# Seven products of a retention layer: four sets of weight buffers, another order at the exchange of passes, and modulation in rows of 1024 columns

## Chip, cores and metric

The kernel runs on one core of one Trainium2 chip. Its time is the device time of one execution in microseconds; a kernel's time is the median over its runs. One execution is also recorded by the hardware profiler, and all readings of the trace are of that one.

## What is computed

Two decoder layers over 512 tokens of width 2048, in float32. Layer 0 is a retention layer with 8 heads (256 wide for queries and keys, 512 wide for values and gates); layer 1 is latent attention. Each layer's input is normalised and modulated: a shift, a scale and a gate come from a product of the conditioning vector with a 2048 x 6144 matrix per layer.

```python
c_act = jax.nn.silu(c)
for i in range(DEPTH):                      # 2 layers
    mod = (c_act @ ada_w[i] + ada_b[i])[:, None, :]
    shift, scale, gate = jnp.split(mod, 3, axis=-1)
    h = rmsnorm(x, norm_g[i]) * (1.0 + scale) + shift
    y = retention_branch(...) if i % 2 == 0 else mla_branch(...)
    x = x + gate * y
return rmsnorm(x, final_norm_g)

def retention_branch(h, pos, w_in, gn_g, w_out):
    proj = h @ w_in                          # 2048 x 12288: q, k (2048 each), v, g (4096 each)
    q, k, v, g = jnp.split(proj, [RET_QK, 2 * RET_QK, 2 * RET_QK + RET_WIDTH], axis=-1)
    q = rope(q, pos); k = rope(k, pos) * RET_DK ** -0.5
    y = chunkwise_retention(q, k, v)         # 8 heads, chunks of 128 tokens
    y = groupnorm(y) * gn_g
    return (silu(g) * y) @ w_out             # 4096 x 2048

def mla_branch(h, pos, w_in, ...):
    cq, ckv, k_rope, g = split(h @ w_in)     # 512, 512, 64, 2048 columns
    ...                                      # attention over 16 heads
    return (silu(g) * o) @ w_out
```

## The kernel before

Every matrix product is made of three matmuls: both operands are split into a high and a low part in a reduced format (`split`: ScalarE casts the high part, VectorE subtracts it to get the low part), and TensorE adds high x high, high x low and low x high. A weight block therefore goes through a raw buffer (a DMA from the chip's memory), a high and a low buffer; `load_w` does this for plain products. Buffers come from pools by tag with a number of places: `raw`, `whi` and `wlo` have three each, `raw2` three more, `tmp` six. PSUM has four banks `acc` and four `aux`. The program is written in one order; a scheduler then orders the instructions of each engine, and each engine runs its own in that order.

The order of the work: the first pass (queries and keys of head 0, values of head 0, three of four column blocks of its gate, while layer 0's shift and scale are computed); a short stage `g03` for the fourth block; then heads 1 to 7. Queries and keys of a head (`queries_and_keys`) are eight units of 24 matmuls. Values and gates of a head (`values_and_gates`) are a 2 x 2 block product done with seven block products rather than eight: tokens in two halves, columns in values and gates, and the 2048 rows in eight pairs of 128-row blocks. Sums and differences of the activations are formed once (`form_sums`); those of the weights are formed by VectorE for each block. *Pass A* has eight units: each loads the rows of a pair (`e`, in a `raw` buffer, and `o`, in a `raw2` buffer; values and gates side by side), forms three differences, splits, and multiplies into the bank pairs `x`, `s`, `y`, `z` (24 matmuls). At the *exchange* ScalarE copies `x` and `s` away (`m1`, `m5`), VectorE adds `m1` to `y` and then `y + m5` to `s`, and `z` is copied (`m4`). *Pass B* has eight units of 18 matmuls: the odd block again (`p`) and the even block's gates (`q`), multiplied into `x`, `s`, `y`. At the end the results go to the chip's memory.

Beside this work runs the rest of the modulation (`later_modulation`): layer 0's gate, layer 1's shift, scale and gate, 16 pieces of 512 columns. A piece is eight 512 KB transfers (two rows of blocks each, buffer `bw`, two places), each followed by two VectorE steps of 512 columns that add the row times its element of the conditioning vector to `am`. `use_modulation` then sums over partitions by small matmuls into `mod_ps` (L532 for shift and scale, L537 for the gates). `next(later, None)` issues one transfer with its two steps; it is called once per unit of `g03`, of queries and keys and of both passes.

After head 7's values and gates come the query and key products of heads 6 and 7, into which `hooks` puts steps of the retention of heads 0 and 1 (loads and rotations by `rope_halves`, the scores `s`, and so on) at given units; then the output projection with the other heads' retention (also by `hooks`), and layer 1: its input `h2`, the low-rank products `cq` and `ckv`, the gates `g2` in four parts, attention, output projection.

Of the kernel before, what the change touches and what calls it, by code (L numbers as in the profile page):

```python
# [16 lines left out]
P = 128  # L17
T = 512
# [31 lines left out]
def hybrid_trunk_kernel(  # L50
# [225 lines left out]
    def rotary_tables(cos, sin, col, signed, name):  # L276

        pos_i = base.tile([P, T], I32, tag="pos", bufs=1, name=f"{name}_pi")
# [210 lines left out]
    def keep_rows(ps, dst_d, r0, name, func=AF.Identity):  # L489
# [8 lines left out]
    def later_modulation():  # L498
        for i, sect, part in (
            [(0, 2, n) for n in range(4)]  # L500
            + [(1, 0, n) for n in range(4)]
            + [(1, 1, n) for n in range(4)]
            + [(1, 2, n) for n in range(4)]
        ):
            name = f"mod_{i}_{sect}_{part}"
            c0 = sect * D + part * 512
            am = lpp.tile([P, T], F32, tag="bm", bufs=2, name=f"{name}_am")
            for u in range(8):
                aw = lpp.tile([P, 2, T], F32, tag="bw", bufs=2, name=f"{name}_aw{u}")
                nc.sync.dma_start(aw, (ada0, ada1)[i][:, 2 * u : 2 * u + 2, c0 : c0 + 512])  # L510
                for ki in range(2):
                    k = 2 * u + ki
                    if k == 0:
                        DVE.tensor_scalar(
                            out=am, in0=aw[:, 0, :], scalar1=cact[:, 0:1], scalar2=None, op0=ALU.mult
                        )
                    else:
                        DVE.scalar_tensor_tensor(  # L518
                            out=am, in0=aw[:, ki, :], scalar=cact[:, k : k + 1], in1=am, op0=ALU.mult, op1=ALU.add
                        )  # L520
                if u == 7:
                    ripe.append((name, i, sect, part, am))
                yield

    def use_modulation():

        while ripe:
            name, i, sect, part, am = ripe.pop(0)
            ps = aux(f"{name}_ps")
            if sect < 2:  # L530
                for b in range(4):
                    PE.matmul(ps[:, b : b + 1], am[:, b * P : (b + 1) * P], crow, start=True, stop=True)  # L532
# [756 lines left out]
```

## Time and profile before

| | |
|---|---|
| median of 3 runs | 2357.36 us |
| lowest and highest run | 2350.77 and 2358.31 us |
| the profiled execution's own time | 2360.03 us |
| its span in the trace | 2357.8 us |
| mean granted clock of TensorE | 0.977 |
| HBM read, written | 396.46 MB, 50.35 MB |

The stages in the profiled execution, by the first matmul of each: first pass 0 to 183 us; `g03` and queries and keys of head 1 to 247.6; then heads 1 to 7, with queries and keys ahead of values and gates up to head 5, to 1046.7; queries and keys of heads 6 and 7 to 1177.4; output projection of layer 0 to about 1605; layer 1 to the end.

How to read it: a matmul's busy time is modelled, and weight loads of TensorE overlap it, so a busy TensorE is measured best by how many matmuls a stretch holds. A wait is put down to the engine and line that released it last. The granted clock is a share of full speed, averaged over the stretch.

### The profile page before, as it was taken

How to read it: one execution, taken by the hardware profiler on the slowest of the kernel's cores; microseconds unless marked ns; L12 is line 12 of the kernel's file. 1: busy time of each engine (PE TensorE's matmuls, PEld its weight loads, DVE VectorE, ACT ScalarE, POOL GpSimd, SP SyncE). 2: the span in 40 equal slices, each digit the busy share in tenths (PEclk: the TensorE clock that was granted, in tenths of full speed). 3: DMA queues.
4: the chain of work that ended last, by engine and by line, in shares of the span. 5: the costliest groups of instructions: out<-in, count | busy, mean ns of one | idle time of the engine just before them, and what ended most of it. 6: DMA issues, size and time to landing. Idle time of an engine off the chain costs nothing.

```text
span 2357.8 us, 28090 instructions
## 1 busy us (share of the span) xinstructions
PE 2229.0 (95%) x10186; PEld 1832.7 (78%) x10186; DVE 1522.9 (65%) x2373; ACT 1008.5 (43%) x1515; POOL 125.7 (5%) x228
## 2 busy tenths in 40 slices
PE   5999999999999899999899999999999999999997
PEld 4777877777778677777688888787888888888886
DVE  6889968677787866766556567347242257777545
ACT  5563433423233244443345455446232255555333
POOL 0000010000000000010000000001000000000000
PEclk8999999999999999999899999999999999999999
DMA  9977888686888865665555454453334333324433
GB/s 323 330 224 241 291 289 268 218 269 219 274 272 304 267 203 178 215 212 186 180 184 177 163 181 138 150 188 108 90 90 134 108 107 99 90 76 165 163 122 119
DMA packets 259500, 448.67 MB, mean 190 GB/s; under 512 B 21913, under 2 KB 95777, under 8 KB 259361
## 3 DMA queue, kind: packets, MB, share of 16 engines
q1 hardware_dynamic: 244256, 400.62, 53.0%
q0 software_dynamic: 14592, 46.18, 5.1%
q8 instruction: 79, 1.29, 0.2%
q14 instruction: 61, 0.49, 0.1%
q10 hardware_dynamic: 512, 0.08, 0.0%
HBM read 396.46 MB, written 50.35 MB: 190 GB/s over the span
## 4 chain that ended last, share of the span: by engine, by line
PE 46%; issue 27%; DMA 11%; DVE 9%; ACT 4%; POOL 2%; SPq 0%; ACTq 0%; POOLq 0%; DVEq 0%
PE o L160 5%; PE o L162 5%; PE o L161 5%; DMA mod_aw<-in_ada_w_dram 5%; PE g L160 2%; PE g L162 2%; PE g L161 2%; DVE mod_am L518 2%; DMA aw<-in_ada_w_dram 2%; DVE am L399 1%; PE qk L162 1%; PE qk L161 1%; PE qk L160 1%; ACT p L1113 1%; DMA qk_raw<-in_ret_w_in_dram 1%
## 5 line engine op out<-in xcount | busy, mean ns | idle before, releaser
L160 PE MATMUL o<-o_w_hi,o_h 128*128 128x512 f32 x768 | 301.7, 393 | 2.7 <-ACT o L881 2.1
L161 PE MATMUL o<-o_w_lo,o_h 128*128 128x512 f32 x768 | 300.0, 391 | 0.0
L162 PE MATMUL o<-o_w_hi,o_l 128*128 128x512 f32 x768 | 298.6, 390 | 0.0
L135 DVE TENSOR_TENSOR o_w_lo<-o_w_raw,o_w_hi 128x1024 fp32r<-128x1024 f32 x96 | 117.2, 1222 | 161.5 <-ACT o_w_hi L134 161.4
L518 DVE SCALAR_TENSOR_TENSOR mod_am<-mod_aw,cact,mod_am 128x512 f32<-128x512 f32 x240 | 179.4, 747 | 46.3 <-DMA mod_aw<-in_ada_w_dram 44.4
L160 PE MATMUL qk<-hT,qk_hi 128*128 128x512 f32 x448 | 180.2, 402 | 4.4 <-ACT qk_hi L134 4.4
L162 PE MATMUL qk<-hT,qk_lo 128*128 128x512 f32 x448 | 177.5, 400 | 0.1
L161 PE MATMUL qk<-hT,qk_hi 128*128 128x512 f32 x448 | 177.4, 396 | 0.0
L160 PEld LDWEIGHTS o<-o_w_hi,o_h 128*128 128x128 f32 x768 | 144.7, 188 | 34.3 <-ACT o L881 4.1
L162 PEld LDWEIGHTS o<-o_w_hi,o_l 128*128 128x128 f32 x768 | 144.2, 188 | 30.5 <-DVE o_l L135 0.6
L161 PEld LDWEIGHTS o<-o_w_lo,o_h 128*128 128x128 f32 x768 | 144.7, 188 | 29.1
L134 ACT CAST o_w_hi<-o_w_raw 128x1024 fp32r<-128x1024 f32 x96 | 100.9, 1052 | 113.5 <-PE o L162 92.8
L134 ACT CAST qk_hi<-qk_raw 128x1024 fp32r<-128x1024 f32 x64 | 67.1, 1051 | 143.9 <-PE qk L161 102.5
L135 DVE TENSOR_TENSOR g_lo<-g_raw,g_hi 128x1024 fp32r<-128x1024 f32 (+1 forms) x42 | 49.2, 1173 | 116.9 <-ACT g_hi L134 108.2
L134 ACT CAST vg_o_hi<-vg_o 128x1024 fp32r<-128x1024 f32 x56 | 59.0, 1053 | 132.3 <-PE s L623 66.6
L160 PEld LDWEIGHTS qk<-hT,qk_hi 128*128 128x128 f32 x448 | 86.3, 193 | 24.5 <-ACT qk_hi L134 5.2
L162 PEld LDWEIGHTS qk<-hT,qk_lo 128*128 128x128 f32 x448 | 85.9, 192 | 20.4 <-DVE qk_lo L135 1.9
L161 PEld LDWEIGHTS qk<-hT,qk_hi 128*128 128x128 f32 x448 | 86.0, 192 | 19.1 <-issue 1.2
L160 PE MATMUL g<-h,g_hi 128*128 128x512 f32 x256 | 99.8, 390 | 1.1 <-ACT ckv_n L994 1.1
L135 DVE TENSOR_TENSOR o_l<-o_in,o_h 128x1024 fp32r<-128x1024 f32 x40 | 48.9, 1224 | 79.8 <-ACT o_h L134 79.7
L162 PE MATMUL g<-h,g_lo 128*128 128x512 f32 x256 | 99.6, 389 | 0.0
L161 PE MATMUL g<-h,g_hi 128*128 128x512 f32 x256 | 99.6, 389 | 0.0
(425 smaller groups left out, 5461.0 us busy)
## 6 DMA issues: line engine op xcount, KB each, us to landing
mod_aw<-in_ada_w_dram SPq DMA_DIRECT2D x128, 512.0 KB, 4.7
aw<-in_ada_w_dram SPq DMA_DIRECT2D x128, 256.0 KB, 6.0
qk_raw<-in_ret_w_in_dram SPq DMA_DIRECT2D x128, 256.0 KB, 4.2
o_w_raw<-in_ret_w_out_dram SPq DMA_DIRECT2D x64, 512.0 KB, 3.8
vg_o<-in_ret_w_in_dram SPq DMA_DIRECT2D x56, 512.0 KB, 5.0
vg_e<-in_ret_w_in_dram SPq DMA_DIRECT2D x56, 512.0 KB, 4.5
vg_p<-in_ret_w_in_dram SPq DMA_DIRECT2D x56, 512.0 KB, 4.2
g_raw<-in_mla_w_in_dram SPq DMA_DIRECT2D x32, 512.0 KB, 3.6
```

What stands on the lines that cost most here:

```text
L134: ACT.copy(hi, src)
L135: DVE.tensor_sub(lo, src, hi.bitcast(F32))
L160: PE.matmul(o, lhs[0], rhs[0], start=first and not seeded, stop=False, skip_group_check=seeded)
L161: PE.matmul(o, lhs[0], rhs[1], start=False, stop=False, skip_group_check=seeded)
L162: return PE.matmul(o, lhs[1], rhs[0], start=False, stop=last, skip_group_check=seeded)
L399: DVE.scalar_tensor_tensor(out=am, in0=aw[:, j], scalar=ck, in1=am, op0=ALU.mult, op1=ALU.add)
L518: DVE.scalar_tensor_tensor(out=am, in0=aw[:, ki, :], scalar=cact[:, k : k + 1], in1=am, op0=ALU.mult, op1=ALU.add)
L1113: ACT.activation(p_[:, :n], ps[:, :n], AF.Exp, bias=nb, scale=scale, accum_out=sm)
```

## The change

- **Buffer sets.** In `values_and_gates` raw, high and low buffers of a block now belong together as a set. Three sets are the old `raw`, `whi`, `wlo`; every fourth block takes a set of its own (`own_r`, `own_h`, `own_l`). `raw2` is gone, and `st` has four places instead of five. Casts and subtractions are written in another order: both casts of a unit, then both low parts.
- **Exchange.** The last unit of pass A multiplies into `x`, `y`, `s`, `z` in that order. `m1` is added to `y` before `s` is copied. Pass B's unit 0 multiplies into `x` alone; unit 1 into `x` and then unit 0's and its own `y` and `s`; later units into `x`, `y`, `s`.
- **Modulation.** A piece is 1024 columns: 16 transfers of one row of blocks (512 KB as before), each followed by one VectorE step of 1024 columns. Its matmuls are issued only when `use_modulation` has been called twice more since it was complete. Steps are issued two per unit of queries and keys (heads 2 to 5) and at every second unit of pass B, none in pass A as the program is written. The gate of layer 1 is left to layer 1 itself, beside the gates `g2`.
- **Start.** `form_sums` moves into the units of `g03` and queries and keys of head 1; head 0's gate rows are put by in `tmp` buffers; the positions' table shares `tmp`.
- **Hooks.** Retention of heads 0 and 1 is stepped at other units of the query and key products of heads 6 and 7, and head 1's rotated rows go to buffers of their own (`odd`); one table of the output projection changes too.

```diff
@@ keep_rows, later_modulation, use_modulation
-        st = lpp.tile([P, T], F32, tag="st", bufs=5, name=name)
+        st = lpp.tile([P, T], F32, tag="st", bufs=4, name=name) if own is None else own(name)
...
-            c0 = sect * D + part * 512
-            am = lpp.tile([P, T], F32, tag="bm", bufs=2, name=f"{name}_am")
-            for u in range(8):
-                aw = lpp.tile([P, 2, T], F32, tag="bw", bufs=2, name=f"{name}_aw{u}")
-                nc.sync.dma_start(aw, (ada0, ada1)[i][:, 2 * u : 2 * u + 2, c0 : c0 + 512])
-                for ki in range(2):
...
+            c0 = sect * D + part * 1024
+            am = pool.tile([P, 2, T], F32, tag="bm", bufs=2, name=f"{name}_am")
+            for k in range(KD):
+                aw = pool.tile([P, 2, T], F32, tag="bw", bufs=2, name=f"{name}_aw{k}")
+                nc.sync.dma_start(
+                    aw, (ada0, ada1)[i][:, k : k + 1, c0 : c0 + 1024].rearrange("p k (a n) -> p (k a) n", a=2)
+                )
+                ck = cact[:, k : k + 1]
+                if k == 0:
+                    DVE.tensor_scalar(out=am, in0=aw, scalar1=ck, scalar2=None, op0=ALU.mult)
+                else:
+                    DVE.scalar_tensor_tensor(out=am, in0=aw, scalar=ck, in1=am, op0=ALU.mult, op1=ALU.add)
+                if k == KD - 1:
+                    ripe.append((clock[0], name, i, sect, part, am))
                 yield
...
+    def use_modulation(age=2):
+        clock[0] += 1
+        while ripe and clock[0] - ripe[0][0] >= age:
...
+    later = later_modulation(lpp, [(i, s_, n) for i, s_ in ((0, 2), (1, 0), (1, 1)) for n in range(2)])
@@ g03
-        each=lambda i: next(later, None),
+        each=form_sums,
@@ values_and_gates
-        def load(kt, name, tag):
-            raw = (base if tag == "raw" else lpp).tile([P, 2, T], F32, tag=tag, bufs=3, name=name)
...
+        def load(src, name):
+            n = turn[0] = turn[0] + 1
+            shape = [P] + [d for d in src.shape[1:]]
+            pool, tags = (lpp, ("own_r", "own_h", "own_l")) if n % 4 == 0 else (base, ("raw", "whi", "wlo"))
+            raw, hi, lo = (
+                pool.tile(shape, dt, tag=tag, bufs=1 if n % 4 == 0 else 3, name=f"{name}_{tag[-1]}")
+                for tag, dt in zip(tags, (F32, F32R, F32R))
+            )
+            nc.sync.dma_start(raw, src)
+            return raw, hi, lo
...
+            e, eh, el = load(block(2 * u, slice(0, 2)), f"vg{h}_{u}_e")
+            o, oh, ol = load(block(2 * u + 1, slice(0, 2)), f"vg{h}_{u}_o")
             DVE.tensor_sub(e[:, 1, :], e[:, 1, :], e[:, 0, :])
+            ACT.copy(eh, e)
             DVE.tensor_sub(o[:, 1, :], o[:, 1, :], e[:, 1, :])
             DVE.tensor_sub(o[:, 0, :], o[:, 0, :], o[:, 1, :])
+            ACT.copy(oh, o)
+            take_low(e, eh, el)
+            take_low(o, oh, ol)
...
+            forms = [(xb, (0, 0), b11), (sb, 1, t1), (yb, 2, t2), (zb, (1, 1), t4)]
+            if u == KD // 2 - 1:
+                forms = [forms[i] for i in (0, 2, 1, 3)]
...
         m1 = [put_by(xb[b], f"m1_{h}_{b}") for b in range(2)]
-        m5 = [put_by(sb[b], f"m5_{h}_{b}") for b in range(2)]
         for b in range(2):
             DVE.tensor_add(yb[b], yb[b], m1[b])
+        m5 = [put_by(sb[b], f"m5_{h}_{b}") for b in range(2)]
         for b in range(2):
             DVE.tensor_add(sb[b], yb[b], m5[b])
...
             product(xb, (1, 0), u, b21, False)
-            product(sb, 4, u, b22, False)
-            product(yb, 3, u, t3, False)
+            held.append((u, b22, (eh, el)))
+            for u_, b22, t3 in held if u > 0 else ():
+                product(yb, 3, u_, t3, False)
+                product(sb, 4, u_, b22, False)
+            if u > 0:
+                held = []
             yield
@@ heads 1 to 7
-    def qk_each(i):
+    def qk_each(i, h):
         use_modulation()
-        next(later, None)
+        if h == 1:
+            if i + 2 < KD // 2:
+                form_sums(i + 2)
+        else:
+            more(2)
+    def vg_each(i):
+        if i >= KD // 2 and i % 2 == 0:
+            more()
...
-        run(values_and_gates(h), each=more)
+        run(values_and_gates(h), each=vg_each)
@@ heads 6 and 7
-    for n, h in enumerate((6, 7)):
-        r_ = retention(n, k4)
+    r_ = (retention(0, k4), retention(1, k4, odd))
+    for h, table in (
+        (6, {0: r_[:1], 3: r_[:1], 5: r_, 7: r_[:1]}),
+        (7, {1: r_[1:], 3: r_[1:], 5: r_[1:]}),
+    ):
...
-        queries_and_keys(h, hooks({0: (r_,), 2: (r_,), 4: (r_,), 6: (r_,)}), qk_keep)
+        queries_and_keys(h, hooks(table), qk_keep)
@@ layer 1
+    later = later_modulation(l2p, [(1, 2, n) for n in range(2)])
     for gi in range(4):
...
@@ g2_each
+            use_modulation()
+            more()
```

More of the change, by code (lines that the diff above doesn't have):

```diff
@@ L561, in hybrid_trunk_kernel, with more @@
+    later = later_modulation(lpp, [(i, s_, n) for i, s_ in ((0, 2), (1, 0), (1, 1)) for n in range(2)])
+    def more(n=1):
+        for _ in range(n):
+            next(later, None)
     H = T // 2
@@ L720, in rope_halves, with retention @@
         split(t3, dst2[:, 0, :], dst2[:, 1, :])
-    def retention(h, own):
+    def retention(h, own, own2=None):
         def fetch(src_d, r0, tag, bufs, name):
@@ L1092, in hybrid_trunk_kernel @@
         )
+    for _ in later:
+        pass
+    use_modulation(0)
     cqT, ckvT = lowT["q"], lowT["kv"]
```

132 lines of the change are left out of this document (55 added, 77 removed).

## The prediction

> **What bounds the kernel now.** First the page's line of busy times, for the engine with the highest share:
>
> ```profile
> PE 2229.0 (95%) x10186; PEld 1832.7 (78%) x10186; DVE 1522.9 (65%) x2373; ACT 1008.5 (43%) x1515; POOL 125.7 (5%) x228
> ```
>
> TensorE works 95% of the span; nothing else is near. So a change here can win only what TensorE loses. For that I read the windows cut at the stages of the layer-0 projections: start; then for heads 1 to 5 queries and keys, pass A, pass B in turn; for heads 6 and 7 the two passes alone; last the two query/key stages of heads 6 and 7, and a stretch each of the output projection's end and of layer 1. The columns are the stretch, its length, busy time (and instructions) of TensorE, of its weight loads, VectorE, ScalarE, GpSimd, then granted clock, share of the DMA engines, GB/s.
>
> ```profile
> 183.30:247.60 64.30, 59.79 (x244) 46.95 (x243) 59.52 (x103) 24.21 (x37) 5.59 (x11) 0.95 0.72 240
> 247.60:291.10 43.50, 43.50 (x194) 36.02 (x193) 43.50 (x57) 20.22 (x23) 1.16 (x3) 1.00 0.87 299
> 291.10:325.10 34.00, 34.00 (x150) 27.66 (x148) 24.98 (x34) 16.38 (x22) 3.12 (x6) 1.00 0.83 272
> 325.10:377.50 52.40, 47.40 (x197) 37.84 (x196) 39.44 (x54) 11.32 (x14) 5.19 (x10) 0.93 0.82 265
> 377.50:425.00 47.50, 45.26 (x193) 35.47 (x192) 39.63 (x50) 19.35 (x22) 1.09 (x2) 1.00 0.82 276
> 425.00:465.50 40.50, 37.35 (x161) 30.61 (x159) 23.21 (x30) 17.15 (x23) 2.67 (x5) 0.92 0.63 194
> 465.50:516.00 50.50, 47.71 (x202) 39.29 (x202) 37.66 (x53) 10.62 (x13) 2.93 (x6) 0.93 0.82 271
> 516.00:564.80 48.80, 46.05 (x193) 35.33 (x192) 39.99 (x50) 19.34 (x22) 0.84 (x2) 1.00 0.82 271
> 564.80:603.20 38.40, 36.26 (x161) 29.80 (x161) 23.24 (x30) 17.23 (x23) 2.67 (x5) 0.96 0.67 203
> 603.20:653.00 49.80, 46.46 (x202) 38.10 (x202) 38.21 (x55) 10.60 (x14) 2.95 (x6) 0.97 0.83 271
> 653.00:706.80 53.80, 48.87 (x202) 38.99 (x201) 44.57 (x60) 19.14 (x22) 0.82 (x2) 0.94 0.84 277
> 706.80:741.10 34.30, 34.24 (x154) 27.92 (x153) 27.66 (x38) 16.68 (x23) 3.22 (x6) 1.00 0.91 304
> 741.10:786.00 44.90, 44.90 (x197) 36.61 (x196) 34.69 (x49) 11.10 (x14) 4.49 (x9) 1.00 0.82 274
> 786.00:839.40 53.40, 46.44 (x194) 36.27 (x193) 44.37 (x56) 19.40 (x22) 0.80 (x2) 0.97 0.78 255
> 839.40:875.30 35.90, 33.57 (x146) 26.78 (x144) 23.41 (x31) 15.83 (x22) 1.53 (x3) 1.00 0.63 186
> 875.30:924.50 49.20, 46.16 (x194) 36.77 (x193) 34.60 (x42) 20.67 (x24) 2.76 (x6) 0.97 0.64 208
> 924.50:960.70 36.20, 33.64 (x146) 26.74 (x144) 23.11 (x31) 15.79 (x22) 1.53 (x3) 1.00 0.61 186
> 960.70:1009.80 49.10, 46.50 (x193) 36.88 (x192) 34.98 (x42) 20.57 (x24) 2.76 (x6) 0.97 0.62 204
> 1009.80:1046.70 36.90, 34.32 (x149) 27.54 (x149) 22.69 (x29) 17.07 (x23) 3.21 (x6) 1.00 0.54 171
> 1046.70:1177.40 130.70, 117.44 (x536) 96.87 (x535) 78.87 (x128) 48.24 (x73) 13.93 (x24) 0.96 0.60 201
> 1600.00:1650.00 50.00, 45.01 (x219) 35.93 (x218) 36.35 (x74) 34.92 (x69) 4.89 (x9) 0.97 0.29 96
> 1750.00:1800.00 50.00, 50.00 (x222) 41.41 (x221) 12.51 (x12) 11.89 (x13) 2.20 (x4) 1.00 0.38 115
> ```
>
> The last row is a stretch without loss: 222 matmuls in 50.00 us, 0.2252 us each at full clock. A query/key stage and a pass A have 192 matmuls (eight units of 24), 43.2 us; a pass B 144 (eight of 18), 32.4 us. Against that the four query/key stages (52.40, 50.50, 49.80, 44.90) lose 24.6 us, the seven passes A (43.50 to 49.10) 42.6, the seven passes B (34.00 to 36.90) 29.2, and the start (64.30 for 244 matmuls) 9.3: some 106 us. What is lost lies where the clock is under 1.00 and where TensorE's busy time falls short of the length. What it waits for, from the waits of TensorE between 183 and 1178 us (total us, times, longest):
>
> ```profile
> PE s L160 <- ACT qk_0p L134: 12.3, 3, 9.6
> PE s L621 <- DVE s L647: 12.0, 5, 3.2
> PE mod_ps L532 <- DVE mod_am L518: 10.3, 3, 4.2
> PE x L622 <- DVE vg_e_lo L135: 7.5, 10, 1.6
> PE y L622 <- DVE vg_o_lo L135: 6.7, 10, 3.3
> PE mod_ps L537 <- DVE mod_am L518: 5.0, 1, 5.0
> ...
> PE z L621 <- DVE m L668: 4.0, 4, 2.0
> ```
>
> Behind the wait of the retention scores (s L160) come the two that this change is about: the second pass of a head waits for the accumulator `s` that VectorE corrects at the exchange of passes (12.0 us in five heads), and the small modulation matmuls wait for their column sum (10.3 and 5.0). Next are the low halves of weight blocks arriving late on VectorE (7.5 and 6.7), and the `z` bank still being read at the next head's start (4.0). The lower clock follows these: 425.00 to 465.50 opens with such an exchange and has 0.92; 291.10 to 325.10 has no loss of this kind and 1.00.
>
> **The change part by part.** Working times of the pieces, from the groups of VectorE and ScalarE between 183 and 1047 us (operation, count, total busy, mean ns) and the DMA issues (KB, us to landing):
>
> ```profile
> L518 DVE SCALAR_TENSOR_TENSOR mod_am<-mod_aw,cact,mod_am 128x512 f32<-128x512 f32 x239 | 178.6, 747 | 46.3 <-DMA mod_aw<-in_ada_w_dram 44.4
> ...
> L135 DVE TENSOR_TENSOR vg_o_lo<-vg_o,vg_o_hi 128x1024 fp32r<-128x1024 f32 x56 | 68.3, 1220 | 2.9 <-ACT vg_o_hi L134 2.9
> ...
> L627 DVE TENSOR_TENSOR vg_e<-vg_e 128x512 f32<-128x512 f32 x56 | 38.5, 687 | 20.0 <-DMA vg_e<-in_ret_w_in_dram 20.0
> ```
>
> ```profile
> L134 ACT CAST vg_o_hi<-vg_o 128x1024 fp32r<-128x1024 f32 x56 | 59.0, 1053 | 132.3 <-PE s L623 66.6 <-DVE vg_o L630 49.1 <-PE qk L161 8.8
> ```
>
> ```profile
> mod_aw<-in_ada_w_dram SPq DMA_DIRECT2D x128, 512.0 KB, 4.7
> ...
> vg_o<-in_ret_w_in_dram SPq DMA_DIRECT2D x56, 512.0 KB, 5.0
> ...
> vg_p<-in_ret_w_in_dram SPq DMA_DIRECT2D x56, 512.0 KB, 4.2
> ...
> g_raw<-in_ret_w_in_dram SPq DMA_DIRECT2D x2, 512.0 KB, 6.2
> ```
>
> *Modulation and the query/key stages.* Pieces are now 1024 wide, and the modulation's matmuls come two units after their sum is complete. In the instruction order of the built program each of them stands tens of microseconds of TensorE work behind its last VectorE step, so the waits of 10.3 and 5.0 go. The longest of the three, 4.2, lies in head 4's pass A (653.00); the other 11.1 us lie in query/key stages. The clock that follows is worth there 0.07 x 52.4 + 0.07 x 50.5 + 0.03 x 49.8 = 8.7 us at most, and about half of it fell into the waits themselves: 4.5. Together some 15.5 of 24.6. The remaining 9 is mostly the small matmuls themselves, which stay. As the hooks also shift the head's first block, I take **-15** (bounds -6, if only half the waits go, and -18).
>
> *VectorE in pass A.* A 1024-wide modulation step isn't in the trace. Between the 1024-wide subtraction's 1.22 and twice 0.747 = 1.49, I take 1.28: 0.747 plus what 512 more columns add to a subtraction (1.220 - 0.687). The built order puts 13, 12, 12 and 13 of these among the weights of passes A of heads 1 to 4, and none in heads 5 to 7. A pass A has 24 steps of 0.69 and 16 of 1.22 = 36 us for the weights, so heads 1 to 4 get 36.1 + 13 x 1.28 = 52.7 us by single durations; in 653.00 to 706.80 some 60 instructions (36.1 + 20 x 0.747 = 51) show 44.57 us busy, as ends overlap, so 52.7 means between 46 (the same overlap) and 52.7; I take 48. TensorE needs 43.2. The difference, 5, must come out of the lead: a set is written again when its reader is done, so three sets lead by two places and four by three, a place being half a unit, 2.7 us: 8.1 us instead of 5.4. So 5 fits in, and the waits for `x` and `y` (14.2 us) mostly go in the middle; in head 1 the row 247.60 shows VectorE at 43.50 of 43.50 already, and there it gets more, not less. Left over, estimated: 3 us in each of heads 1 to 4, 1 in each of 5 to 7, 15 of 42.6. With that go the start of heads 6 and 7, where `z` waits (4.0) since the `y` products now end 1.35 us before the pass does, the mod wait in head 4 (4.2 with 0.94 of clock), and in head 5 (53.40, the modulation's last 512-wide pieces) 9 of 10.2. **-27** (bounds -6 and -38).
>
> *The exchange.* Before, the unit after the exchange needed `x`, `s`, `y`; `s` is ready after four additions on VectorE, and TensorE has only six `x` matmuls, 1.35 us, to cover copies and additions. Now the last unit of pass A runs x, y, s, z, so that `x` and `y` are copied 2.7 us before the pass ends, and pass B begins with two units of `x` (12 matmuls, 2.7 us), `y` needed at +2.7 and `s` at +4.05 instead of +1.35. The longest wait was 3.2, so 2.7 more covers all but 0.5 of it. What becomes late instead: the low half of the second unit's block stands behind the four additions on VectorE, and is needed at +2.9; and the difference for the short block, which waits on a DMA (4.2 us from issue), stands ahead of the `y` additions. Either can hold all four additions back: nothing to 3.2 us a head, I take 1.5. 7 x 1.5 = 10.5 and 4 of small things remain of 29.2: **-14.5** (bounds 0 and -25).
>
> *The start.* Sums are now formed inside the short g03 stage, whose g0 rows go to another buffer. The order puts two first-pass modulation transfers and one more block ahead of g03's first block on SP, and rotary tables and the first sums ahead of its low half on VectorE; a 512 KB block took 6.2 us here, plus 1.05 and 1.22 for the halves. So between nothing and 8.5 us are added to the 9.3 lost now: **+3**.
>
> *Heads 6 and 7.* Retention's scores come at units 3, 5, 7 rather than 2, 4, 6, and head 1's rotations into a buffer of their own. Of the 12.3 us behind the rows' halves, 9.6 is one wait for what head 7 has just stored, which stays; the other 2.7 go, with some clock: **-4** (0 to -8).
>
> *Layer 1.* The last two gate pieces, 32 steps, run among the first products of layer 1; some come into the chain of 1600.00 to 1650.00, where VectorE has 36.35 of 50.00 busy; seven there cost up to 7 x 1.28 = 9.0 if all lie on the path, nothing if none: with the two pairs of gate products **+5** (0 to 12).
>
> Sum: 3 - 15 - 27 - 14.5 - 4 + 5 = -52.5 on the profiled execution's 2360.0 us, 2307.5; its time is 2.7 above the median, so **2305 us** to compare with 2357.4. The bounds added up give -95 to +24 and are not all reached together.
>
> By the Trainium skill ("TensorE: Matmul & The Clock Gate", HAM oscillation) only gaps over about 3.4 us drop the clock; then the exchange waits, at most 3.2, would cost none, and the gain would be about 5 us less. The 0.92 of the stretch that opens with the 3.2 us wait speaks against so sharp a limit.
>
> **The rivals.** *Half the gain.* Around pass A of heads 3 and 4 the built order has 16 modulation blocks with 16 weight blocks on SP, 32 x 0.524 = 16.8 MB in 43.2 us. The row 706.80 has 304 GB/s at a share of 0.91; at 1.00 that is 334, and 16.8 MB take 50.3 us. If the transfers have no head start on that (two modulation buffers, four sets), TensorE waits 7.1 us in each of four heads: 2305 + 28 = **2333**. For: VectorE is just as dense there, and before no pass A took over 299 GB/s. Against: only heads 1 to 4, and SP runs ahead. The Trainium skill ("DMA: Bandwidth & Descriptors", Where 436 GB/s comes from) puts HBM per core at about 358 GB/s; by it the blocks take 46.9 us, and the wait is 3.7.
>
> *Slower: four raw blocks instead of six.* Raw, high and low now go by one set, so the raw buffers fall from three and three to four. A raw block's turn is issue and landing, subtractions 1.2, the cast 1.05, two low halves 2.4, minus overlaps, about landing + 4, and two units of pass A allow 10.8; in pass B landing + 2.9 and 8.1. With 5.0 and 4.2 landing that is 9.0 and 7.1: it fits. Landing over 6.8 in A or 5.2 in B makes the turn the bound, and more so, since fewer blocks are under way. At 7.2 it costs 0.4 x 4 turns x 7 heads = 11 and 2.0 x 28 = 56; the time is 2305 + 67 = **2372**. It turns slower from 7.0 on. For: 6.2 was seen at the start, where share is high. Against: 4.2 to 5.0 at shares up to 0.91.
>
> *No change.* The four additions held at every exchange by the late short block, the low halves late again, and the start at its bound: about **2355**.
>
> **How the numbers follow.** The forecast with its bounds 0.58, half the gain 0.22, four raw blocks 0.14, no change 0.06. The measurement of this kernel tells about 0.3%, 7 us, from no change. Faster: 0.58 + 0.21 + 0.01 = 0.80; within: 0.04; slower: 0.16. Range: the forecast's own is 2280 to 2332; below it lies 0.05. At the other end it takes in half the gain, no change and the near part of four raw blocks, and leaves out 0.13: 2280 to 2356.
>
> **What would show it.** Right: no modulation wait on TensorE; s L647 waits under 1 us or replaced by ones for `vg_p_lo`; passes A at 44 to 46 us, query/key stages at 45 to 47, clock 0.99 or more between 250 and 1000 us. Half the gain: passes A of heads 1 to 4 at 49 to 51 at a DMA share of 0.95 or more, the rest as forecast. Four raw blocks: VectorE's idle before the first subtraction of a block ended by its DMA, landings above 6 us, passes B at 38 or more. The prediction is wrong if TensorE's total waits between 183 and 1178 us don't fall to about half.

## The result, and the profile after

The changed kernel takes 2373.69 us (median of 6 runs, 2369.71 to 2384.35) against 2358.22 us (6 runs of the kernel before): a ratio of 1.0071, 95% interval 1.0044 to 1.0097. It is slower by 0.7%, where 2305 us with a range of 2280 to 2356 was forecast. The profiled execution has 2375.32 us and a span of 2373.2. The page's line of busy times:

```profile
PE 2229.5 (94%) x10186; PEld 1835.6 (77%) x10186; DVE 1508.6 (64%) x2247; ACT 1004.7 (42%) x1517; POOL 126.8 (5%) x228
```

TensorE does the same work in the same busy time (2229.0 before), in a span 15.4 us longer. The stages of the changed kernel, with the same columns as before: the start; five of the seven passes A (heads 1 to 4 and 6); five passes B (heads 1, 2, 4, 5, 6); queries and keys of heads 6 and 7; and layer 1 from its first transposes to the gates g2.

```profile
183.30:249.00 65.70, 57.85 (x241) 46.85 (x242) 57.08 (x92) 26.51 (x37) 2.18 (x5) 0.92 0.56 179
249.00:296.30 47.30, 45.00 (x193) 35.63 (x192) 40.74 (x45) 18.07 (x21) 1.30 (x3) 1.00 0.90 303
384.80:438.40 53.60, 45.94 (x193) 36.92 (x193) 46.05 (x50) 19.05 (x23) 3.23 (x6) 0.94 0.82 273
523.40:572.10 48.70, 45.53 (x193) 35.69 (x194) 38.47 (x43) 18.89 (x23) 2.19 (x4) 1.00 0.81 270
657.80:706.20 48.40, 45.52 (x195) 35.63 (x195) 41.68 (x47) 16.95 (x20) 0.88 (x2) 1.00 0.86 295
877.00:924.40 47.40, 45.43 (x193) 37.10 (x193) 35.99 (x45) 21.41 (x26) 3.73 (x7) 0.96 0.69 226
296.30:337.10 40.80, 36.20 (x145) 28.77 (x144) 36.05 (x42) 14.90 (x20) 1.61 (x3) 0.92 0.86 283
438.40:477.80 39.40, 34.69 (x145) 27.96 (x144) 27.25 (x34) 14.75 (x20) 1.47 (x3) 0.96 0.74 235
706.20:745.60 39.40, 35.62 (x145) 28.90 (x144) 31.10 (x36) 14.73 (x20) 0.54 (x1) 0.91 0.79 259
836.80:877.00 40.20, 34.79 (x145) 27.98 (x144) 23.97 (x31) 14.81 (x20) 0.54 (x1) 0.96 0.53 161
924.40:958.70 34.30, 32.97 (x146) 26.96 (x145) 23.25 (x29) 14.84 (x21) 0.60 (x2) 1.00 0.58 183
1047.50:1177.00 129.50, 117.18 (x537) 96.95 (x537) 75.68 (x125) 49.16 (x72) 12.73 (x22) 0.95 0.61 200
1602.90:1739.00 136.10, 120.96 (x537) 96.51 (x535) 98.00 (x141) 59.66 (x108) 9.09 (x14) 0.95 0.66 203
```

A stage runs from its first matmul to the next stage's (the start from 183.3 us in both). By the two traces:

| stage | before | after | change | forecast |
|---|---|---|---|---|
| start (g03, queries and keys 1) | 64.3 | 65.7 | +1.4 | +3 |
| queries and keys, heads 2 to 5 | 197.5 | 185.8 | -11.7 | -15 |
| seven passes A | 345.4 | 339.2 | -6.2 | -27 |
| seven passes B | 256.2 | 273.6 | +17.4 | -14.5 |
| queries and keys 6 and 7 | 130.7 | 129.5 | -1.2 | -4 |
| output projection of layer 0 | 428.4 | 425.9 | -2.5 | 0 |
| layer 1 up to g2 | 121.9 | 136.1 | +14.2 | +5 with g2 |
| g2 | 176.0 | 179.5 | +3.5 | |

The waits of TensorE between 183 and 1178 us:

```profile
PE x L633 <- DVE vg_p_o L627: 24.1, 9, 4.6
PE x L633 <- DVE vg_e_o L627: 16.7, 8, 6.2
PE s L160 <- ACT qk_0p L134: 11.7, 2, 10.4
PE g L160 <- ACT g_hi L134: 7.1, 1, 7.1
PE y L633 <- DVE vg_o_l L627: 4.9, 5, 1.4
PE y L632 <- DVE s L665: 3.1, 1, 3.1
PE x L632 <- ACT qk_st L492: 2.4, 2, 2.2
```

The modulation waits (15.3 us) and those for `s` (12.0) and `z` (4.0) are gone, as forecast. In their place stand 24.1 us for the low half of a block `p` in pass B (`vg_p_o`: the tag's last letter is now part of the name, `w`, `i`, `o` for raw, high and low of the three common sets, `r`, `h`, `l` for the fourth), and 16.7 us rather than 7.5 for that of a block `e` in pass A. The first comes about in two ways. The exchange of head 5 shows the one, which the trace has in heads 3, 5, 6 and 7. VectorE:

```profile
836.79 1.29 DVE L662 TENSOR_TENSOR y<-y,m 128x512 f32<-128x512 f32 x2
839.77 0.69 DVE L672 TENSOR_TENSOR vg_q_w<-vg_p_w,vg_q_w 128x512 f32<-128x512 f32 x1 [1.69 <-DMA vg_q_w<-in_ret_w_in_dram]
840.39 1.29 DVE L665 TENSOR_TENSOR s<-y,m 128x512 f32<-128x512 f32 x2
841.59 1.21 DVE L627 TENSOR_TENSOR vg_p_o<-vg_p_w,vg_p_i 128x1024 fp32r<-128x1024 f32 x1
```

The transfer of unit 2's short block on SP's queue, and TensorE:

```profile
836.90 0.34 SPq L620 DMA_DIRECT2D vg_q_w<-in_ret_w_in_dram  x1
```

```profile
838.13 0.61 PE L632 MATMUL x<-vg_p_i,hT 128*128 128x512 f32 x2
842.85 0.50 PE L633 MATMUL x<-vg_p_o,hT 128*128 128x512 f32 x1 [4.11 <-DVE vg_p_o L627]
```

TensorE has done the first unit of `x` and begins the second at 838.13; it needs the low half of unit 1's block (`vg_p_o`), which VectorE makes at 841.59. Ahead of it VectorE has the `y` additions, then the difference of *unit 2's* short block (L672), for which it waits 1.69 us until the transfer issued at 836.90 lands, then the `s` additions. Nothing that TensorE needs next depends on unit 2.

In heads 1, 2 and 4 unit 2's difference stands behind the low half, and modulation steps stand ahead of it. In head 2 three of them (434.27, 436.60 and 440.12 us) come before the `y` additions; the last, what follows it, and TensorE's wait:

```profile
440.12 1.28 DVE L514 SCALAR_TENSOR_TENSOR mod_am<-mod_aw,cact,mod_am 128x1024 f32<-128x1024 f32 x1 [0.61 <-DMA mod_aw<-in_ada_w_dram]
441.32 1.29 DVE L662 TENSOR_TENSOR y<-y,m 128x512 f32<-128x512 f32 x2
442.51 1.28 DVE L665 TENSOR_TENSOR s<-y,m 128x512 f32<-128x512 f32 x2
443.71 1.21 DVE L627 TENSOR_TENSOR vg_p_o<-vg_p_w,vg_p_i 128x1024 fp32r<-128x1024 f32 x1
```

```profile
444.98 0.80 PE L633 MATMUL x<-vg_p_o,hT 128*128 128x512 f32 x1 [4.61 <-DVE vg_p_o L627]
```

In head 1 such a step stands between the `y` and the `s` additions. Head by head the longest wait for `vg_p_o` is 0.9 to 4.6 us, and in head 1 one of 3.1 for `s` comes on top; the clock of the passes B is 0.91 to 0.96, but for head 6 (1.3 us, 1.00). The passes B one by one, with three of the runs that follow:

| head | 1 | 2 | 3 | 4 | 5 | 6 | 7 |
|---|---|---|---|---|---|---|---|
| before | 34.0 | 40.5 | 38.4 | 34.4 | 35.9 | 36.2 | 36.9 |
| changed | 40.8 | 39.4 | 38.7 | 39.5 | 40.3 | 34.3 | 40.7 |
| e2_q2 | 41.0 | 38.8 | 34.9 | 40.5 | 36.5 | 34.3 | 38.4 |
| e3_both | 38.3 | 35.3 | 38.1 | 34.8 | 33.6 | 33.6 | 37.5 |
| e9_noxq | 40.5 | 38.0 | 34.7 | 39.0 | 33.8 | 32.7 | 35.3 |

### The profile page after: what moved, and what is told of

Same layout as the page of the kernel before. It is cut to its first block, busy times and chain, and to the rows that moved or that the text cites. A ratio compares the mean times of both kernels' runs of the same rounds, so it can differ in the third digit from the quotient of the medians.

```text
span 2373.2 us, 28016 instructions
## 1 busy us (share of the span) xinstructions
PE 2229.5 (94%) x10186; PEld 1835.6 (77%) x10186; DVE 1508.6 (64%) x2247; ACT 1004.7 (42%) x1517; POOL 126.8 (5%) x228
## 4 chain that ended last, share of the span: by engine, by line
PE 47%; DMA 19%; DVE 17%; issue 10%; ACT 5%; POOL 1%; SPq 0%; DVEq 0%; ACTq 0%; POOLq 0%
PE o L160 4%; PE o L161 4%; PE o L162 4%; DMA mod_aw<-in_ada_w_dram 4%; DMA vg_e_w<-in_ret_w_in_dram 3%; DMA vg_o_w<-in_ret_w_in_dram 3%; PE g L160 2%; PE g L161 2%; PE g L162 2%; DMA aw<-in_ada_w_dram 2%; DVE mod_am L514 2%; DMA vg_q_w<-in_ret_w_in_dram 2%; PE qk L162 2%; PE qk L160 2%; PE qk L161 2%
## 5 line engine op out<-in xcount | busy, mean ns | idle before, releaser
L514 DVE SCALAR_TENSOR_TENSOR mod_am<-mod_aw,cact,mod_am 128x1024 f32<-128x1024 f32 x120 | 153.7, 1281 | 47.5 <-DMA mod_aw<-in_ada_w_dram 46.7
L160 PE MATMUL qk<-hT,qk_hi 128*128 128x512 f32 x448 | 175.9, 393 | 1.7 <-ACT qk_hi L134 1.7
L161 PE MATMUL qk<-hT,qk_hi 128*128 128x512 f32 x448 | 174.3, 389 | 0.0
L135 DVE TENSOR_TENSOR qk_lo<-qk_raw,qk_hi 128x1024 fp32r<-128x1024 f32 x64 | 78.0, 1221 | 59.2 <-ACT qk_hi L134 50.2
```

The costliest lines, as they stand in the source:

```text
L135: DVE.tensor_sub(lo, src, hi.bitcast(F32))
L160: PE.matmul(o, lhs[0], rhs[0], start=first and not seeded, stop=False, skip_group_check=seeded)
L161: PE.matmul(o, lhs[0], rhs[1], start=False, stop=False, skip_group_check=seeded)
L514: DVE.scalar_tensor_tensor(out=am, in0=aw, scalar=ck, in1=am, op0=ALU.mult, op1=ALU.add)
```

## Experiments

Two theories were set against each other. *Order*: VectorE runs in the order that the built program gives it, and work of a later unit that waits for a transfer stands there ahead of what TensorE needs first. *Four raws*: with four raw buffers instead of six, transfers come late whatever the order. Sums of passes A and B and "layer 1" (first transposes to g2) are from each run's own trace, one execution each: kernels whose passes B are written alike (changed, e4, e6) have 273.6, 277.8 and 274.0, those whose layer 1 is written alike 133.5 to 136.3, so a few microseconds in such a sum tell nothing by themselves. Ratios are to the kernel before on the same chip (2358.12 us for e1 to e4, 2358.27 for e5 to e8, 2353.83 for e9 to e12) and not quite the quotients of the medians.

| run | median us | ratio and interval | A | B | layer 1 |
|---|---|---|---|---|---|
| changed | 2373.69 | 1.0071 (1.0044 to 1.0097) | 339.2 | 273.6 | 136.1 |
| e1_adds | 2386.80 | 1.0122 (1.0092 to 1.0153) | 340.4 | 279.3 | 134.2 |
| e2_q2 | 2355.79 | 0.9991 (0.9982 to 1.0001) | 333.5 | 264.4 | 136.3 |
| e3_both | 2350.15 | 0.9965 (0.9950 to 0.9981) | 332.7 | 251.1 | 134.8 |
| e4_l2pin | 2362.76 | 1.0014 (0.9999 to 1.0029) | 341.7 | 277.8 | 124.1 |
| e5_nox | 2361.03 | 1.0008 (0.9994 to 1.0021) | 325.9 | 275.6 | 134.2 |
| e6_pina | 2362.05 | 1.0018 (1.0007 to 1.0028) | 328.7 | 274.0 | 134.0 |
| e7_b4 | 2357.40 | 0.9996 (0.9984 to 1.0009) | 350.9 | 249.8 | 121.2 |
| e8_all | 2337.84 | 0.9915 (0.9900 to 0.9930) | 325.0 | 254.2 | 124.7 |
| e9_noxq | 2340.36 | 0.9946 (0.9926 to 0.9965) | 326.7 | 254.1 | 133.5 |
| e10_three | 2385.27 | 1.0135 (1.0114 to 1.0157) | 372.9 | 258.4 | 136.0 |
| e11_s4 | 2350.95 | 0.9990 (0.9972 to 1.0007) | 330.4 | 262.9 | 121.3 |
| e12_best | 2322.85 | 0.9881 (0.9860 to 0.9901) | 324.0 | 252.6 | 124.2 |

**The order at the exchange: e1, e2, e3.** `tc.issue_after(x)` puts what stands under it behind `x` on x's engine. The edits here and below are shortened.

```diff
 e1_adds (the additions leave their place ahead of pass B)
-            take_low(o, oh, ol)
+            low = take_low(o, oh, ol)
+            if u == 1:
+                with tc.issue_after(low.ins):
+                    (y += m1, then s = y + m5, two banks each)
             take_low(e, eh, el)
 e2_q2
-            DVE.tensor_sub(e, o[:, 1, :], e)
+            with tc.issue_after(low.ins) if u >= 2 else nullcontext():    # low of unit u - 1
+                DVE.tensor_sub(e, o[:, 1, :], e)
 e3_both: both, low being the last addition for u == 2
```

> The changed kernel, but at each exchange VectorE does the four additions (m1 to y, then y + m5 to s) right behind the low half of pass B's second odd block (p of unit 1), and not ahead of it. Order theory: the low half that TensorE waits for in pass B (24 us in nine waits) stands behind four additions, 2.4 us, and behind the difference of unit 2's short block, which waits for its transfer; only the first goes, so these waits fall to 8 to 14 us, some of it comes back as waits for the additions, and the time falls by 6 to 14 us against the changed kernel's 2373.7. Four-raws theory (the blocks' transfers come late because four raw buffers turn too slowly, the order does not matter): the waits keep within 4 us of 24 and the time within 4 us.

> The changed kernel, but in pass B the difference of a unit's short block (from unit 2 on) is issued on VectorE behind the low half of the odd block of the unit before; the four additions stay where they are. Order theory: the wait for unit 2's transfer no longer holds the second additions and the low half of unit 1; in the five heads where the trace shows 1.7 us of idle VectorE there and 0.6 of work, about 2.3 us go each, the waits of pass B fall from 27 to 12 to 18 us and the time by 8 to 18 us. Four-raws theory: the lateness only moves to unit 2, whose low halves TensorE then waits for: the waits of pass B stay above 22 us and the time within 4 us.

> Both edits of the two runs before: on VectorE the low half of unit 1's odd block, then the four additions, then the rest, with unit 2's difference behind them. Order theory: pass B's waits fall from 27 us to under 8, its clock comes back to 0.98 or more, the seven passes B take 236 to 245 us together rather than 273.7, and the time is 2336 to 2350. Four-raws theory: the waits move to units 2 and 3, passes B stay above 262 us, the time above 2362.

In e2 nothing but the difference of the short block is moved (from unit 2 on); the ratio falls from 1.0071 to 0.9991 and the time by 17.9 us, at the upper end of what the order theory expected. Half of it lies in the passes B, 9.2 us, and 5.7 in the passes A. But the waits of pass B fell only from 27.2 to 22.4 us, not to 12 to 18. The table by heads shows why: heads 3, 5, 6 and 7 got 9.9 us shorter together, while heads 1, 2 and 4, where modulation steps hold the additions, did not change (119.7 and 120.3) and kept 14.7 us of these waits. No run moves those steps alone, so what they cost is read from the order and the durations (in head 2 an estimate of 3 x 1.28 + 0.61 = 4.5 us ahead of a wait of 4.6). e1 missed, by its sign: in its order the additions do stand behind the low half, but unit 2's difference, which e1 leaves alone, stands ahead of both, so that the late transfer now holds everything; the wait hardly changes:

```profile
PE x L633 <- DVE vg_p_o L627: 22.4, 10, 4.9
```

Its own 13 us were not traced to a cause (the passes B are 5.7 longer, head 3's above all, and queries and keys of head 4 take 52.0 for 47.1). Only both edits take most of the wait away, in heads 1, 2 and 4 too, since the low half now stands ahead of the additions. In e3:

```profile
PE x L632 <- ACT qk_st L492: 10.4, 2, 6.5
...
PE x L633 <- DVE vg_p_o L627: 5.3, 3, 2.8
```

Passes B fall to 251.1, though not to the 236 to 245 expected, the time (2350.15) ends at the top of its range, and a wait grows that the changed kernel had little of (2.4): TensorE starts pass A when ScalarE has copied the query and key banks away (`qk_st`), and these copies stand behind casts whose differences are late on VectorE.

**Layer 1: e4.**

```diff
-            use_modulation()
-            more()
+            if gi > 0:
+                use_modulation()
+                with tc.issue_after(last_low[0].ins):     # the last low half of g2 issued
+                    more(2)
```

> The changed kernel, but layer 1's last two gate pieces are issued on VectorE behind the low halves of the second and later parts of the gates g2, two steps per unit, so none can stand among the steps that make layer 1's input and the low-rank products. Theory: the 15 us that the stretch from the first transposes of layer 1 to the end of g2 lost come from these 32 steps (1.28 us each) and their transfers standing ahead of the chain on VectorE; g2 starts 10 to 13 us after the end of the output projection's loss as before, the four gate matmuls cost 3 us beside g2, and the time falls by 9 to 15 us against 2373.7. Rival: the loss comes from what was left of the chain itself (buffers, another order on ScalarE); then the time stays within 4 us.

In the changed kernel VectorE has these steps in layer 1 before g2 (line L514 alone, 1602.9 to 1739):

```profile
1602.90:1739.00 136.10, 38.47 (x30) 0.95 0.66 203
```

and TensorE waits there for steps of the chain:

```profile
PE x1T L965 <- DVE h2f L982: 4.8, 3, 4.3
PE ckv L160 <- ACT cq_n L1025: 4.2, 2, 2.2
PE kr_ps L160 <- ACT ckv_n L1025: 2.1, 1, 2.1
PE cq L162 <- DVE h L983: 1.3, 1, 1.3
```

With the two first steps of a piece that is all 32 of them. Of these waits the first is not new (3.4 us before, 5.0 in e4); the other three, 7.6 us, are, and e4 has none of them. Behind g2's low halves the steps cost nothing: the stretch is back at 124.1 us, its DMA share at 0.33 from 0.66. g2 keeps its 3.5 us, the gate matmuls. The theory held.

```profile
1602.00:1726.00 124.00, 117.36 (x534) 95.53 (x533) 64.25 (x115) 58.19 (x105) 9.48 (x16) 0.97 0.33 100
```

**The exchange put back: e5, and e9 with e2's edit.**

```diff
-            if u == KD // 2 - 1:
-                forms = [forms[i] for i in (0, 2, 1, 3)]
...
-            held.append((u, b22, (eh, el)))      (and the lines that use held)
+            product(sb, 4, u, b22, False)
+            product(yb, 3, u, (eh, el), False)
 both copies ahead of the additions, as before; e9: and the difference as in e2_q2
```

> The changed kernel with its exchange put back: the last unit of pass A runs x, s, y, z again, both copies come before the additions, and pass B's units run x, s, y from the first. Sets, modulation and hooks stay changed. Order theory: what made passes B longer is that with two units of x first a second low half is needed 1.35 us before anything else, and it stands behind the additions and the late transfer; with the exchange put back TensorE waits for s again, 2 to 3.5 us a head in all seven heads (before: five), and the passes B take 255 to 266 us together rather than 273.6; time 2360 to 2370. Four-raws theory: the turn of the raw buffers makes passes B long whatever the order; they stay above 270 us and the time within 4 us of 2373.7.

> The changed kernel with its exchange put back (as in e5_nox) and, as in e2_q2, unit 2's difference behind the low half of unit 1. It tells what the new order at the exchange is worth once nothing overtakes the additions. If the new order works as it was predicted to, the old one waits here for s again, 2 to 3.5 us in each of seven heads and more than e2_q2 does, and the time is 2358 to 2368 against e2_q2's 2355.8. If the new order is worth nothing or less, since its second unit of x needs a low half that stands behind the same additions and its y ahead of s needs the odd block's low half earlier in pass A, the time is 2338 to 2352.

e5's time (2361.03) fell as the order theory said, but its passes B stay long, as the four-raws theory said. The cause is another: in heads 3, 5, 6 and 7 the same difference now overtakes one of the two `y` additions, and so holds `s`, in head 3:

```profile
567.00 0.69 DVE L661 TENSOR_TENSOR y<-y,m 128x512 f32<-128x512 f32 x1
569.93 0.69 DVE L669 TENSOR_TENSOR vg_q_w<-vg_p_w,vg_q_w 128x512 f32<-128x512 f32 x1 [2.24 <-DMA vg_q_w<-in_ret_w_in_dram]
570.54 0.69 DVE L661 TENSOR_TENSOR y<-y,m 128x512 f32<-128x512 f32 x1
```

```profile
PE s L632 <- DVE s L663: 28.7, 7, 4.7
```

e9 takes it away, and with the old exchange passes B fall to 254.1; of the waits that remain 13.0 us are in heads 1, 2 and 4, where modulation steps stand ahead of the additions here too:

```profile
PE s L632 <- DVE s L663: 16.4, 6, 4.8
```

So with this edit the new order at the exchange is worth less than nothing: 0.9946 with the old one, 0.9991 with the new one. (With the additions moved too, as in e3, the new order has 0.9965; its interval and e9's overlap.) It saves the waits for `s` (16.4 us remain in e9) and makes new ones: a second low half 2.7 us into pass B that stands behind four additions, and `y` ahead of `s` in pass A's last unit, which needs the odd block's low half 1.35 us earlier (4.9 us of waits in the changed kernel; in e5 1.3). Passes A are 13.3 us shorter in e5 than in the changed kernel; how much of this is that one wait and how much the head's start was not separated.

**The order in pass A: e6.**

```diff
+            with tc.issue_after(low_e.ins) if u > 0 else nullcontext():    # low of unit u - 1
                 the three differences of unit u
```

> The changed kernel, but in pass A the three differences of a unit (from the second on) are issued on VectorE behind the low half of the even block of the unit before, so that no difference that waits for a transfer can stand ahead of a low half that is needed earlier. Order theory: the waits of pass A for the even block's low half (16.7 us in eight waits, mostly at the second unit of a head) fall below 8 us, passes A together from 339.2 to 325 to 333, the time by 6 to 14 us. Four-raws theory: the waits come from transfers issued late since a raw buffer is free only when its low half is done; the order changes nothing or makes it worse, since the difference itself now starts later; passes A stay above 336.

The order theory held: passes A 339.2 to 328.7, the time 11.6 us less, and the wait for `vg_e_o` from 16.7 to 8.3 us, just over the 8 expected.

**Raw buffers and the fourth set: e7, e10, e11.**

```diff
 e7_b4 (kernel before): raw blocks in turn over raw, raw, raw, raw2, instead of three raw and three raw2
 e10_three (changed kernel)
-            pool, tags = (lpp, (own...)) if n % 4 == 0 else (base, ("raw", "whi", "wlo"))
+            pool, tags = (base, ("raw", "whi", "wlo"))
 e11_s4 (kernel before): load, casts and low halves of the changed kernel, its exchange undone
```

> The kernel before with four raw buffers in turn instead of three and three; high and low stay three each, all else as before. Four-raws theory: passes A and B get longer by what the changed kernel lost, 15 to 40 us together, and the time is 2372 to 2398. Order theory: with three sets of halves the raw buffers of blocks further ahead were of little use, passes A and B together change by less than 8 us, and the time is 2352 to 2366.

> The changed kernel without its fourth set: raw, high and low three each, all else as changed. In the instruction order of the built program the differences of units 1 and 2 then stand behind the additions of the exchange, and not ahead of them. If the fourth set costs time by letting these differences ahead, passes B get shorter, 273.6 to 255 to 268 us together; passes A get longer by the lost lead, 339 to 342 to 360; time 2365 to 2385. If passes B are long for another reason, they stay above 270 us, and the time is above 2378.

> The kernel before with the four sets alone (and their order of casts and low halves); exchange, modulation, start and hooks as before. In the built order unit 2's difference stands ahead of the additions in heads 5 to 7, and not in head 2. If the sets give their lead to pass A and cost it at the exchange where a difference overtakes: passes A 345 to 325 to 338 us, waits for s of 3.5 to 5 us in heads 5 to 7 and as before in the others, passes B 256 to 256 to 266, time 2342 to 2358. If the sets alone make the passes B long: over 268 us, time 2360 or more.

e7 decides against four raws as a cause by itself: the kernel before loses nothing with four (passes A +5.5, B -6.4, ratio 0.9996). Nor were transfers slower in the changed kernel:

```profile
vg_e_w<-in_ret_w_in_dram SPq DMA_DIRECT2D x56, 512.0 KB, 4.5
vg_p_w<-in_ret_w_in_dram SPq DMA_DIRECT2D x56, 512.0 KB, 3.9
```

The issue-to-landing times of 4.5 and 3.9 us are those of before (4.5 and 4.2). e10 shows what the fourth set gives: without it the passes A are 372.9 us, more than expected. (It has only three raw buffers, where the kernel before has six, so the 33.7 us between the two are not a gain over the kernel before.) But the passes B are 258.4: with three sets the differences stand behind the additions in the built order. e11 shows both at once on the kernel before: passes A 15.0 us shorter, and passes B 40.3, 38.3 and 40.4 us in heads 5 to 7 (before 35.9, 36.2, 36.9), just where unit 2's difference overtakes (head 5: 2.83 us of idle VectorE), while heads 1 to 4 have 144.1 (before 147.3).

```profile
838.62 0.69 DVE L666 TENSOR_TENSOR vg_q_w<-vg_p_w,vg_q_w 128x512 f32<-128x512 f32 x1 [2.83 <-DMA vg_q_w<-in_ret_w_in_dram]
```

So it is with the fourth set that a later unit's difference gets ahead. That it is placed there because its buffers are free is argued, not shown; in the changed kernel it happens only in the four heads without modulation steps at the exchange.

**All together: e8 and e12.** e8 has e3, e4 and e6; e12 one order more:

```diff
+            with tc.issue_after(last_st[0].ins) if u == 1 else nullcontext():   # the last copy of the qk banks
                 ACT.copy(oh, o)
```

> The changed kernel with the orders of runs e3_both, e4_l2pin and e6_pina together. If the three losses are independent: 23.5 less from the exchange (2373.7 to 2350.2), 11 less from layer 1 (2362.8) and 5 to 12 from pass A: 2327 to 2336. If the order in pass A makes no difference: 2337 to 2342.

> Run e8_all with one more order: on ScalarE the cast of the second odd block of a head stands behind the four copies that empty the banks of queries and keys. In e8_all TensorE waited 13.5 us for these copies at the start of pass A in three heads, since casts stood ahead of them whose differences came late. If the copies were only held by that cast, the waits fall below 4 us and the time to 2322 to 2330; if VectorE is late there with modulation steps in any case, the wait moves to the second unit's low half and the time stays at 2333 to 2340.

e8 came to 2337.84, 2 us above the range that independent losses would have given, and in the one named for an order in pass A that makes no difference. That order did work (passes A are 7.7 us shorter than in e3); three stages fell (A 325.0, B 254.2, layer 1 124.7), but the wait behind ScalarE's casts ate part of it:

```profile
PE x L636 <- ACT qk_st L494: 13.5, 3, 6.2
```

e12 takes it away; queries and keys of heads 2 to 5 are 176.3 us, down from e8's 191.9. The first three waits of e12:

```profile
PE s L162 <- ACT qk_0p L136: 12.9, 2, 10.4
PE g L162 <- ACT g_hi L136: 8.0, 1, 8.0
PE x L639 <- DVE vg_p_o L633: 6.1, 5, 1.9
```

At 2322.85 us (ratio 0.9881, 0.9860 to 0.9901) it beats both kernels, with every part of the change kept and only the places of some instructions changed. (It lies in the range expected, 2322 to 2330; but that was reckoned from runs on chips where the kernel before took 2358 us, and here it took 2353.83.) The two longest waits left are one that the change did not touch, the retention scores at head 7's end, and one that it made, at the start.

## Why the prediction was wrong, point by point

- **What bounds the kernel**: right; TensorE's busy time is the same (2229.5 and 2229.0 us), and what was lost lies in its waits. The sign that the text named for being wrong came: the waits between 183 and 1178 us rose from 64 to 72 us, where about half was to be left.
- **The bounds**: added up wrongly. The six terms' bounds give -89 to +8.5, not -95 to +24. The stages of the table came out at +14.9, above the right sum, so at least one bound had to fail; those of the exchange and of layer 1 did.
- **Modulation and query/key stages** (-15): -11.7. The waits went. What ate the rest is a new wait for `qk_st` (2.2 us) in front of head 2's pass A, and small modulation matmuls that stayed (9.1 us of TensorE's time in the four stages). The 1024-wide step was sized right: 1.28 us was taken, and measured is

```profile
L514 DVE SCALAR_TENSOR_TENSOR mod_am<-mod_aw,cact,mod_am 128x1024 f32<-128x1024 f32 x90 | 115.2, 1280 | 29.7 <-DMA mod_aw<-in_ada_w_dram 29.2
```

- **The exchange** (-14.5): the step that failed most, by 31.9 us: +17.4, outside its bounds of 0 and -25. The text named two dangers, the low half behind the additions and a difference waiting for its transfer, and then took 1.5 us a head of "nothing to 3.2". The waits are 1.3 to 5.4 us a head. In heads 3, 5, 6 and 7 both dangers come together and in one queue, and the difference is not only unit 1's but unit 2's, which has no need to be there, and whose transfer is issued only when unit 0's set is free; e2 brings 9.9 us back in these heads. In heads 1, 2 and 4 modulation steps stand at the exchange, which the text's term for the passes B leaves out; heads 1 and 4 have +6.8 and +5.1 of the +17.4. e3, which puts the low half ahead of the additions, brings back 22.5 in all. Behind it stood a wrong premise, that `y` is needed at +2.7 and `s` only at +4.05: the `s` additions read `y`, so TensorE cannot add to `y` before they are done, and all four are due at +2.7. Head 1 has that wait (3.1 us of `y` for `s`). The text took waits for the low half of `p` in place of those for `s` as a sign of being right; they came, with 24.1 us for 12.0.
- **VectorE in pass A** (-27): failed by 20.8. The lead of four sets is real (e11: 15.0 us against the kernel before), and VectorE's load did not reach the estimate: in the passes A of heads 1 to 4 it was busy 40.7, 46.1, 38.5 and 41.7 us, where 48 was taken. But a head's second or third unit does not have it: its low half stands behind a later unit's difference, which e6 shows with 10.5 us, and `y` ahead of `s` in the last unit adds 4.9 us of waits.
- **Layer 1** (+5, 0 to 12): +17.7. Seven steps were counted in the chain of layer 1's input; the low-rank products behind it, up to g2, are a chain on VectorE too, and all 32 steps stood there. The bound was made from the first part alone. e4 confirms it with 12 us of 14.2.
- **Start** (+3): +1.4, by luck. TensorE waits 7.1 us for g03's first block, as the text feared, and g03 takes 15.9 us for 10.9, together more than the bound of 8.5; but queries and keys of head 1 take 43.7 us for 53.4, which the text did not count. What made them shorter was not tested.
- **Heads 6 and 7** (-4): -1.2, within its bounds. The one long wait stayed (10.4 us), and of the other 2.7 us 1.3 stayed. The output projection's -2.5 was not forecast.
- **The rivals**: "four raw blocks" gave 2372, close to what was measured, but by another mechanism: landings did not rise, and e7 shows no loss. Two of its three signs did come, passes B at 38 us or more (six of seven) and VectorE idle ahead of a difference until its transfer lands; they did not tell it from a wrong order. "No change" named the right place (additions held by the late short block) at a price of some 50 us instead of the 68.7 by which the result lies above the forecast. "Half the gain" did not occur: it asked for a DMA share of 0.95 or more in the passes A of heads 1 to 4, which have 0.90, 0.82, 0.81 and 0.86.
- **The clock**: by a rule of the Trainium skill ("TensorE: Matmul & The Clock Gate", HAM oscillation) TensorE should have no idle gaps over about 3.4 us. The prediction weighed whether shorter ones cost nothing; the last section shows a shorter one that was followed by a drop.

## What to carry to other kernels

More buffers do not only give lead: with them a scheduler can place work of a later unit ahead of what is needed now, and on an engine that runs its queue in order one such instruction that waits for a transfer holds all behind it. After adding a buffer, read the new order at every exchange, and ask of each instruction that waits for a transfer what stands behind it; one fixed order (e2) was worth as much as the whole change lost. Work moved "out of the way" can come to stand in any chain on its engine, as the modulation steps did in layer 1 (e4) and, by the order, at three exchanges; so count all its instructions in every dependent chain up to the place where it is wanted. And when an accumulator is needed earlier, look for what else still reads it.

## What the runs showed of the hardware that was not expected

A wait of 2 us can be followed by half the clock. TensorE's wait at head 6's second unit in the changed kernel, and the stretches before and after it (columns as above):

```profile
884.85 0.66 PE L633 MATMUL x<-vg_e_o,hT 128*128 128x512 f32 x1 [1.97 <-DVE vg_e_o L627]
```

```profile
877.00:885.00 8.00, 6.03 (x27) 4.67 (x27) 6.54 (x11) 5.33 (x8) 3.73 (x7) 1.00 0.97 370
884.00:894.00 10.00, 9.15 (x33) 7.44 (x34) 8.34 (x10) 3.08 (x4) 0.00 (x0) 0.83 0.76 261
```

The clock is 1.00 up to 885 and 0.83 over the ten microseconds from 884 on; the matmuls there follow each other at 0.45 and 0.43 us (884.85, 885.30, 885.73) instead of 0.2252. The length of the wait does not decide alone: one of 2.20 us in the same trace (384.76) and two of 2.27 and 2.58 in the kernel before (843.17, 1013.94) were not followed by a drop, the granted clock being 1.00 over 380 to 390 us, 843 to 853 and 1013 to 1023. What decides is open. The first of the two rows shows, too, that 370 GB/s at a DMA share of 0.97 were moved in 8 us, more than the 334 that the prediction worked out for a full share.
